# LayerNorm boundaries in another order: weight units of the modulation behind the statistics, four at each boundary, and the next two weight units split ahead

## The chip, the core and the metric

The kernel runs on one core of a Trainium2 chip. Its engines are TensorE (PE; its weight loads are shown as PEld), VectorE (DVE), ScalarE (ACT), GpSimd (POOL) and SyncE (SP, which issues most of the weight transfers). Each of them works through its own list of instructions in the order in which the list was written; the lists meet through semaphores. The metric is the device time in microseconds (us) of one execution.

## What is computed

The reference runs a trunk of four layers over 288 token columns: a prompt of 256 tokens and eight samples of 4. Cut to what matters:

```python
for i in range(DEPTH):                      # DEPTH = 4, d = 1024
    mod = sc @ w_ada[i] + b_ada[i]          # sc = silu(c): 9 vectors, w_ada[i] is 1024 x 6144
    sh1, sc1, g1, sh2, sc2, g2 = jnp.split(mod[:, None, :], 6, axis=-1)
    h = x * (1 + sc1) + sh1
    out = mixer(i % 3, h)                   # 0: gating MLP, 1: gated recurrence, 2: latent attention
    x = layer_norm(ALPHA * x + g1 * out, ln1_g[i], ln1_b[i])
    h = x * (1 + sc2) + sh2
    x = layer_norm(ALPHA * x + g2 * squared_relu_mlp(h, w1[i], w2[i]), ln2_g[i], ln2_b[i])
```

All is in 32-bit floats. The layers 0 and 3 have the gating MLP as their mixer, layer 1 the recurrence, layer 2 the attention.

## The kernel before

Activations lie with the 1024 features on partitions, in 8 chunks of 128, and the 288 tokens along the free dimension. A large matmul is done as three (`mm3`, L271 to L276): each operand is split into a high part and a low part, and high x high, low weight x high and high x low are added up in PSUM. So before a product the activation needs `Hi` and `Lo`, and each weight needs `hi` and `lo`.

Weights come in units of 1 MB: 1024 rows by 256 columns. `set_plan` fixes the order of all units. `load_next` issues a unit's transfer on SP into one of five `raw` buffers, and buffers are given back in the order of the plan only. `pump_` splits a unit in pieces of 1024 columns: ScalarE writes `hi` (L229), VectorE writes `lo` (L230). There are three pairs of `hi` and `lo`. `run_units` multiplies: a pair of units gives four output tiles. At the start of a stage (`inter=True`) the first two units are multiplied chunk by chunk of the activation, so that the matmuls of chunk 0 can start as soon as chunk 0 of `Hi` and `Lo` is there.

The modulation's matrix `w_ada` (24 MB a layer) also goes through the `raw` buffers, in 24 units a layer (each 1 MB): `ada` units and `adh` units. A unit is four matmuls of 32 columns by 512 (`ada_step`, L476), straight from `raw` without a split; the trace shows two records for each matmul, eight for a unit. After a group of units the sum is copied from PSUM by ScalarE (`adas`), turned by small matmuls on TensorE (L497 or L511) and added to a bias by VectorE. Where the units of the modulation stand in TensorE's list is set by three things: when their buffer must be free, the flag `hold`, and `fence`, a matmul behind which they must stand. Before the change `fence` is the last weight matmul ahead of a LayerNorm, and `ada_need` forces groups at certain places (ahead of the output projection of a mixer, and behind a boundary).

A boundary (`boundary`, L697) is the LayerNorm between two stages; there are seven, and a last one with the output (`store_y`). From the last matmul of a stage it goes: VectorE adds the residual to the last chunk of `Z`, ScalarE squares it, four matmuls with a constant matrix give mean and mean square over the features (`stats`, L611 to L614), ScalarE and VectorE make the reciprocal root (`rstd`: `va`, logarithm, exponential, and one correction step, L633 to L635). Then for each chunk VectorE subtracts the mean (L646) and multiplies (L649), ScalarE and VectorE write `Hi` (L661, L663) and a 32-bit copy `hf`, and VectorE writes `Lo` (L669). The scheduler of the language orders the instructions by dependencies and priority; `issue_after` adds a dependence without data, and `low` lowers a priority.

Of the kernel before, what the change touches and what calls it, by code (L numbers as in the profile page):

```python
# [11 lines left out]
AF = mybir.ActivationFunctionType  # L12
# [34 lines left out]
FENCE = 1  # L47

# [3 lines left out]
class Net:  # L52
    def __init__(s, ctx, tc, I, O, layers):
        s.tc, s.nc, s.I, s.O = tc, tc.nc, I, O
        s.layers = layers
        s.ctx = ctx
        P = lambda name, bufs=1, **k: ctx.enter_context(tc.tile_pool(name=name, bufs=bufs, **k))
        s.cst = P("cst")
        s.raw = P("raw", RAWB)
        s.hip = P("hip", HLB)  # L60
        s.lop = P("lop", HLB)
        s.acp = P("act")
        s.table = None
# [4 lines left out]
        s.paced = []  # L68

# [24 lines left out]
    def set_plan(s, plan):  # L94
# [7 lines left out]
        s.hold = True  # L102
        s.quiet = False
        s.rs_ins = None
# [65 lines left out]
    def pump(s, force=False):  # L170
        if s.quiet and not force:
            return False
        if s.rs_ins is not None and not force:
            with s.tc.issue_after(s.rs_ins), s.low(SPLIT_LATER):
# [96 lines left out]
    def mm3(s, out, w, x, first, last):  # L271

        mm = s.nc.tensor.matmul
        mm(out, w[0], x[0], start=first, stop=False)  # L274
        mm(out, w[1], x[0], start=False, stop=False)  # L275
        s.last_mm = mm(out, w[0], x[1], start=False, stop=last).ins  # L276
# [16 lines left out]
    def run_units(s, keys, x, evac, m0=0, nk=8, inter=False, kgroups=1, quiet=False):  # L293
# [4 lines left out]
        if inter:  # L298
# [3 lines left out]
            for k in range(nk):  # L302
                for m in range(4):
                    with s.after(k + 1):
                        s.mm3(pss[m][:, :T], s.wtile(ws[m // 2], k, m % 2), x(k), k == 0, k == nk - 1)
                    if k == nk - 1:
                        if m % 2:
                            s.wfree(ks[m // 2])
                        evac(m0 + m, pss[m])
# [288 lines left out]
    def stats(s, Z):  # L598
# [15 lines left out]
        nc.tensor.matmul(pq[:, :T], s.onesD, sq, start=False, stop=True)  # L614
        return pm, pq

    def rstd(s, pq, sub, out, n=T, mul=1.0):
# [3 lines left out]
        if sub is not None:  # L621
            nc.vector.scalar_tensor_tensor(v, pq, EPS, sub, op0=OP.add, op1=OP.subtract)
# [14 lines left out]
    def normalize(s, Z, pm, pq, each):  # L637
# [6 lines left out]
        if s.quiet:  # L644
            s.rs_ins, s.quiet = ins, False
        sub = lambda c: nc.vector.tensor_tensor(Z[:, c, :], Z[:, c, :], pm[:, :T], op=OP.subtract)  # L646
        for c in range(NCH):
            sub(c)
            nc.vector.tensor_tensor(Z[:, c, :], Z[:, c, :], rs, op=OP.mult)  # L649
            each(c)  # L650

    def make_h(s, Z, sub, c):
# [11 lines left out]
        nc.scalar.activation(hf[:, p], Z[:, c, p], AF.Identity, scale=A[:, c, 0:1], bias=B[:, c, 0:1])  # L664
        nc.vector.tensor_tensor(v(hf[:, q]), v(tp), bc(B), op=OP.add)
# [21 lines left out]
    def residual(s, Z, g, b, m):  # L687
# [5 lines left out]
        for c in range(NCH):  # L693
            nc.vector.tensor_scalar(s.AX[:, c, :], Z[:, c, :], ga[:, c:c + 1], ga[:, 8 + c:9 + c],
                                    op0=OP.mult, op1=OP.add)

    def boundary(s, sub, i):  # L697

        pm, pq = s.stats(s.Z)
# [21 lines left out]
    def ffn(s, i):  # L721
# [3 lines left out]
        with s.tc.tile_pool(name=f"ffn{i}", bufs=1) as fp:  # L725
# [16 lines left out]
            for h in range(2):  # L742
# [3 lines left out]
                if h == 0:  # L746
                    s.run_units(keys, y, lambda m, ps: s.gated(s.AX[:, m, :], ps, g, m), kgroups=2)
                else:
                    s.hold = True
# [899 lines left out]

    def before_out(s, i):  # L1650
        if i != s.layers[0]:
            s.ada_need(("adh", i, 4, 3))
            if i != s.layers[-1]:
                s.ada_need(("adh", i, 5, 3))
        s.hold = True

    def run(s):
# [3 lines left out]
        for n, i in enumerate(L):  # L1661
# [11 lines left out]
        s.set_plan(plan)  # L1673
        s.setup()
        s.late_setup()
        for n, i in enumerate(L):
            first, last = n == 0, n + 1 == len(L)
            s.hold = False
            if n:
                s.ada_need(("ada", i, 1, 7))  # L1680
                s.hold = True
# [11 lines left out]
            if first:  # L1693
                s.later_setup()
            if first or last:
                s.ada_need(("adh", i, 5, 3))
            if not last:
                i1 = L[n + 1]
                s.ada_need(("ada", i1, 0, 7))
                s.prep_ab(i1, 0, s.lnv(2, i), s.lnv(3, i))  # L1700
# [97 lines left out]
```

## Time and profile before

| | us |
|---|---|
| median of 3 runs | 1626.4 (1622.16 to 1628.55) |
| the profiled execution, its own time | 1626.94 |
| its span, first to last instruction | 1625.2 |
| TensorE busy in it | 1580.1 |
| VectorE busy | 1025.6 |
| ScalarE busy | 798.2 |

The span is that of the same execution as the trace, so rows of the trace are set against 1625.2, and 1.7 us lie around it. A busy time is the union of an engine's instructions; matmuls overlap, so on TensorE the distance from start to start says more than the length of one. A wait is the idle time of an engine ahead of an instruction, put down to what ended it.

### The profile page before, as it was taken

Reading aid. Unit: us, or ns where it says so; the run is one execution under the profiler, and the core shown is the slowest. Engines: PE = TensorE matmul, PEld = TensorE weight load, DVE = VectorE, ACT = ScalarE, POOL = GpSimd, SP = SyncE. Lnnn points to the kernel's source line nnn. Section 1 sums busy time; section 2 is a strip of 40 time slices with the busy share of each in tenths; the row PEclk is TensorE's granted clock in tenths of the full one; section 3 lists DMA queues with packets and bytes.
Section 4 is the critical chain, followed back from the end, with each engine's and each line's share of the span. In section 5 each row is a group of like instructions: output and inputs, shape, how many; then the busy total and the mean of one; then the engine's idle time right before and its main releaser. Section 6 shows DMA issues by size and latency. Waiting matters only on the chain.

```text
span 1625.2 us, 30504 instructions
## 1 busy us (share of the span) xinstructions
PE 1580.1 (97%) x12538; PEld 1402.2 (86%) x12538; DVE 1025.6 (63%) x2290; ACT 798.2 (49%) x1436; POOL 53.0 (3%) x70
## 2 busy tenths in 40 slices
PE   6999999999999989999999999999999999899997
PEld 2878899997989769999987676779999799799997
DVE  3567855656778786555676344586466775874655
ACT  2554643545777655345364453455254464553542
POOL 1000000000101100000002210000000000000000
PEclk9999999999999999999999999999999999999999
DMA  9977955458555868555465447696554766655531
GB/s 332 331 268 243 340 172 165 158 180 291 163 159 164 300 253 260 164 160 177 156 214 178 158 168 252 215 310 208 159 172 162 258 209 211 207 182 175 162 105 42
DMA packets 222717, 332.58 MB, mean 205 GB/s; under 512 B 7171, under 2 KB 196041, under 8 KB 213362
## 3 DMA queue, kind: packets, MB, share of 16 engines
q1 hardware_dynamic: 215954, 299.86, 55.6%
q0 software_dynamic: 6624, 30.78, 5.7%
q8 instruction: 98, 1.61, 0.4%
q14 instruction: 41, 0.34, 0.1%
HBM read 324.09 MB, written 6.53 MB: 203 GB/s over the span
## 4 chain that ended last, share of the span: by engine, by line
PE 90%; DMA 5%; DVE 3%; ACT 1%; issue 0%; SPq 0%; DVEq 0%; ACTq 0%
PE mm L274 24%; PE mm L276 23%; PE mm L275 23%; PE ada L476 5%; DMA raw<-in_w_ada 3%; PE mm L1408 2%; DMA raw<-in_ffn_w 1%; PE mx L1426 1%; PE mm L1462 1%; PE mx L815 1%; PE mx L1480 1%; PE mx L917 1%; PE mx L1430 1%; PE ada L530 1%; DVE lo L230 1%; PE mm L1508 1%
## 5 line engine op out<-in xcount | busy, mean ns | idle before, releaser
L230 DVE TENSOR_TENSOR lo<-raw,hi 128x1024 fp32r<-128x1024 f32 x360 | 433.2, 1221 | 166.5 <-ACT hi L229 166.0
L229 ACT ACTIVATE hi<-raw 128x1024 fp32r<-128x1024 f32 x360 | 370.6, 1053 | 264.1 <-PE mm L276 191.0
L274 PE MATMUL mm<-Hi,hi 128*128 128x288 f32 x1064 | 318.5, 300 | 1.8 <-ACT Hi L1161 0.9
L275 PE MATMUL mm<-Hi,lo 128*128 128x288 f32 x1064 | 316.7, 298 | 0.0
L276 PE MATMUL mm<-Lo,hi 128*128 128x288 f32 x1064 | 315.0, 298 | 0.0
L276 PE MATMUL mm<-FL,hi 128*128 128x288 f32 x1024 | 303.6, 297 | 0.0
L274 PE MATMUL mm<-FH,hi 128*128 128x288 f32 x1024 | 302.6, 296 | 0.0
L275 PE MATMUL mm<-FH,lo 128*128 128x288 f32 x1024 | 298.6, 292 | 0.0
L274 PEld LDWEIGHTS mm<-Hi,hi 128*128 128x128 f32 x1064 | 199.8, 188 | 19.6 <-issue 10.1
L274 PE MATMUL mm<-OH,hi 128*128 128x288 f32 x704 | 209.6, 299 | 2.7 <-ACT OH L661 2.7
L275 PE MATMUL mm<-OH,lo 128*128 128x288 f32 x704 | 208.8, 297 | 0.2 <-DVE lo L230 0.2
L276 PEld LDWEIGHTS mm<-Lo,hi 128*128 128x128 f32 x1064 | 199.5, 188 | 10.3 <-issue 8.4
L275 PEld LDWEIGHTS mm<-Hi,lo 128*128 128x128 f32 x1064 | 199.9, 188 | 9.4 <-issue 8.6
L276 PE MATMUL mm<-OL,hi 128*128 128x288 f32 x704 | 207.2, 297 | 0.0
L275 PEld LDWEIGHTS mm<-FH,lo 128*128 128x128 f32 x1024 | 195.2, 191 | 0.0
L274 PEld LDWEIGHTS mm<-FH,hi 128*128 128x128 f32 x1024 | 192.4, 188 | 0.0
L276 PEld LDWEIGHTS mm<-FL,hi 128*128 128x128 f32 x1024 | 191.9, 187 | 0.0
L737 ACT ACTIVATE r<-mm 128x288 f32<-128x288 f32 x128 | 52.3, 412 | 175.2 <-PE mm L276 159.0
L274 PEld LDWEIGHTS mm<-OH,hi 128*128 128x128 f32 x704 | 132.9, 189 | 5.5 <-ACT OH L661 3.6
L276 PEld LDWEIGHTS mm<-OL,hi 128*128 128x128 f32 x704 | 132.8, 190 | 4.3 <-issue 3.4
L275 PEld LDWEIGHTS mm<-OH,lo 128*128 128x128 f32 x704 | 133.2, 189 | 1.4 <-issue 0.8
L739 DVE TENSOR_TENSOR s<-r 128x288 f32<-128x288 f32 x128 | 58.1, 456 | 103.6 <-ACT r L737 103.5
(434 smaller groups left out, 2073.4 us busy)
## 6 DMA issues: line engine op xcount, KB each, us to landing
raw<-in_ffn_w SPq DMA_DIRECT2D x128, 1024.0 KB, 5.6
raw<-in_w_ada SPq DMA_DIRECT2D x88, 1024.0 KB, 5.6
raw<-in_a_w_in SPq DMA_DIRECT2D x16, 1024.0 KB, 9.2
raw<-in_b_w_in SPq DMA_DIRECT2D x16, 1024.0 KB, 8.5
raw<-in_w_ada SPq DMA_DIRECT2D x16, 512.0 KB, 10.0
raw<-in_a_w_out SPq DMA_DIRECT2D x8, 1024.0 KB, 5.9
St<-in_state_hgrn POOLq DMA_DIRECT2D x8, 512.0 KB, 6.4
out_hs_s<-St POOLq DMA_DIRECT2D x8, 512.0 KB, 4.1
```

The costliest lines, as they stand in the source:

```text
L229: nc.scalar.activation(hi[:, a:b], r[:, a:b], AF.Copy)
L230: nc.vector.tensor_tensor(lo[:, a:b], r[:, a:b], hi[:, a:b].bitcast(F32), op=OP.subtract)
L274: mm(out, w[0], x[0], start=first, stop=False)
L275: mm(out, w[1], x[0], start=False, stop=False)
L276: s.last_mm = mm(out, w[0], x[1], start=False, stop=last).ins
L476: nc.tensor.matmul(s.pa[32 * j:32 * j + 32, :], x, w, start=(k == 0), stop=(k == last), skip_group_check=True)
L530: mm = nc.tensor.matmul(pa[r0:r0 + 32, :], s.scT[:, 2 * kp + par, :], t[:, par, h, :], start=(kp == 0), stop=(kp == 3), skip_group_check=True)
L737: nc.scalar.activation(r, ps[:, :T], AF.Relu)
L739: nc.vector.tensor_tensor(sq, r, r, op=OP.mult)
L815: nc.tensor.matmul(pt[:, 128 * q:128 * q + 128], vt01[:, q, sl], s.wsT[:, c, :], start=True, stop=True)
L917: mm(pt[32 * b:32 * b + 32, 64 * hh + 32 * g:64 * hh + 32 * g + 32], k[:, hh, a:a + 32], q[:, hh, a:a + 32], start=True, stop=True, skip_g ...
L1408: tr(pt[:, 128 * n:128 * n + 128], lat[b][t // 8][:, t % 8, 128 * c:128 * c + 128], s.id)
```

## The change

- Modulation units at a boundary: `fence` becomes the last matmul of the statistics, and after each weight unit the last matmul of that unit. A counter `quota` lets four units go at a boundary (`FILL`), and then one for each weight unit that is done; `alim` bounds how far ahead they may run.
- The plan of units is laid out to fit: two weight units, four modulation units, and then one modulation unit after each weight unit in the mixers, after every second one in the MLP (`spread`). The groups that were forced ahead of the output projections of layers 1 and 2 are no longer there.
- `presplit` splits the next stage's first two weight units ahead of the statistics.
- `normalize`: three subtractions of the mean go right behind `va`, the others behind the reciprocal root; chunk 0 goes to its end ahead of the others; further splits wait for chunk 4 of `h`, and the residual copy `AX` for the last chunk.
- `run_units` at the start of a stage: for all chunks but the last, the two matmuls with `Hi` of all four tiles, then the one with `Lo`.
- The constants and tables that were made at the first boundary (`later_setup`) move into the first MLP.

```diff
+EARLY = 3
+AHEAD = 4
+FILL = 4
+SPACE = (1, 1, 1)
...
+    def presplit(s):
+
+        while s.nsplit < min(s.wdone + 2, len(s.wlist)):
+            s.reach(s.wlist[s.nsplit])
+            s.pump(force=True)
...
         s.wdone += 1
         del s.hl[key]
+        s.quota = max(s.quota, 0) + 1
+        s.fence = s.last_mm
         s.advance()
...
             for k in range(nk):
+                if k < nk - 1:
+                    for part in range(2):
+                        for m in range(4):
+                            with s.after(k + 1):
+                                s.mm3(pss[m][:, :T], s.wtile(ws[m // 2], k, m % 2), x(k), k == 0, False, (part,))
+                    continue
...
-        if s.ndone >= len(s.alist) or s.alist[s.ndone] >= s.nd or (s.hold and not force):
+        if s.ndone >= len(s.alist) or s.alist[s.ndone] >= s.nd or ((s.hold or s.quota < 1 or
+                                                                                s.alist[s.ndone] > s.alim) and not force):
             return False
+        s.quota -= 1
...
+        with s.tc.issue_after(s.va_ins):
+            for c in range(EARLY):
+                sub(c)
+        front, s.h_ins = ins, None
         for c in range(NCH):
-            sub(c)
-            nc.vector.tensor_tensor(Z[:, c, :], Z[:, c, :], rs, op=OP.mult)
-            each(c)
+            with s.tc.issue_after(front):
+                if c >= EARLY:
+                    sub(c)
+                nc.vector.tensor_tensor(Z[:, c, :], Z[:, c, :], rs, op=OP.mult)
+                each(c)
...
     def boundary(s, sub, i):
 
+        s.presplit()
         pm, pq = s.stats(s.Z)
...
+    def spread(s, w, a, first, n, step):
+
+        out, a = list(w[:first]) + list(a[:n]), list(a[n:])
+        for k, u in enumerate(w[first:]):
+            out.append(u)
+            if a and k % step == step - 1:
+                out.append(a.pop(0))
+        return out + a
+
     def before_out(s, i):
         if i != s.layers[0]:
             s.ada_need(("adh", i, 4, 3))
-            if i != s.layers[-1]:
-                s.ada_need(("adh", i, 5, 3))
+        s.hold = True
...
-                plan += s.merge(a, s.ada_units(i, 1), *R1) + s.merge(o, sc2 + ([] if last else g2), *R2)
-            fill = (g2 if first or last else []) + ([] if last else s.ada_units(L[n + 1], 0))
-            plan += s.merge(f[0] + f[1], fill, *R0[n]) + f[2] + f[3]
+                plan += s.spread(a, s.ada_units(i, 1) + sc2, 2, FILL, SPACE[i % 3]) + o
+            fill = g2 + ([] if last else s.ada_units(L[n + 1], 0))
+            plan += s.spread(f[0] + f[1], fill, 2, FILL, 2) + f[2] + f[3]
...
-            if FENCE:
-                s.fence = s.last_mm
             s.boundary(1, i)
-            s.hold = False
...
+            s.fence = s.last_stat
+            s.hold, s.quota = False, FILL
...
+            s.advance()
+            s.ada_need(("adh", i, 5, 3))
+            s.quota = 0
             s.rs_ins = None
             s.ffn(i)
             if not last:
-                if FENCE:
-                    s.fence = s.last_mm
                 s.boundary(0, i)
+                s.fence = s.last_stat
```

Three places in the instruction lists follow. The first is TensorE's list at the second boundary, that between the MLP of layer 0 and the recurrence of layer 1; `ada<-raw` are matmuls of modulation units, four to a unit, and `mx<-zs`, `mx<-sqs`, `mx<-Z` and `mx<-sq` are the statistics. Before:

```order
L611 MATMUL mx<-zs,con 128x288
L612 MATMUL mx<-sqs,con 128x288
L476 MATMUL ada<-raw,scT 32x512
L613 MATMUL mx<-Z,con 128x288
L614 MATMUL mx<-sq,con 128x288
L476 MATMUL ada<-raw,scT 32x512 x23
L274 MATMUL mm<-Hi,hi 128x288
```

The same place now:

```order
L639 MATMUL mx<-zs,con 128x288
L640 MATMUL mx<-sqs,con 128x288
L641 MATMUL mx<-Z,con 128x288
L642 MATMUL mx<-sq,con 128x288
L504 MATMUL ada<-raw,scT 32x512 x16
L294 MATMUL mm<-Hi,hi 128x288
```

The one unit matmul between the statistics is gone, and four units instead of six stand ahead of the first weight matmul. The second place is TensorE's list in the last part of the recurrence in layer 1, where the matmuls of the last pair of heads (`q,k`, `St,q`, `con,k`) follow one another and the weight matmuls have become few. Before:

```order
L476 MATMUL ada<-raw,scT 32x512
L969 MATMUL mx<-q,k 32x32 x8
L476 MATMUL ada<-raw,scT 32x512 x8
L982 MATMUL mx<-q,k 64x64 x4
L476 MATMUL ada<-raw,scT 32x512 x7
L274 MATMUL mm<-Hi,hi 128x288
L990 MATMUL mx<-q,k 128x128 x2
L998 MATMUL mx<-St,q 32x512 x4
```

The same place now:

```order
L1017 MATMUL mx<-q,k 32x32 x8
L294 MATMUL mm<-Hi,hi 128x288
L295 MATMUL mm<-Hi,lo 128x288
L1030 MATMUL mx<-q,k 64x64 x4
L1038 MATMUL mx<-q,k 128x128 x2
L1046 MATMUL mx<-St,q 32x512 x4
```

The units have gone from between the heads' matmuls. The third place is VectorE's list at the third boundary, that between the recurrence and the MLP of layer 1; `lo<-raw,hi` is a piece of a split, `Z<-gs,AX` the end of the residual sum of the last chunk, `Z<-Z,mx` a subtraction of the mean. Before:

```order
L573 TENSOR_TENSOR gs<-mm,modT_81 128x32
L230 TENSOR_TENSOR lo<-raw,hi 128x1024
L574 TENSOR_TENSOR Z<-gs,AX 128x32
L230 TENSOR_TENSOR lo<-raw,hi 128x1024
L646 TENSOR_TENSOR Z<-Z,mx 128x288
L622 SCALAR_TENSOR_TENSOR va<-mx,msq 128x288
L646 TENSOR_TENSOR Z<-Z,mx 128x288 x3
L633 SCALAR_TENSOR_TENSOR vl<-rs,va 128x288
L646 TENSOR_TENSOR Z<-Z,mx 128x288
L634 TENSOR_TENSOR vl<-vl,rs 128x288
L646 TENSOR_TENSOR Z<-Z,mx 128x288
L635 SCALAR_TENSOR_TENSOR rs<-vl,rs 128x288
```

The same place now:

```order
L601 TENSOR_TENSOR gs<-mm,modT_81 128x32
L241 TENSOR_TENSOR lo<-raw,hi 128x1024
L602 TENSOR_TENSOR Z<-gs,AX 128x32
L650 SCALAR_TENSOR_TENSOR va<-mx,msq 128x288
L674 TENSOR_TENSOR Z<-Z,mx 128x288 x3
L661 SCALAR_TENSOR_TENSOR vl<-rs,va 128x288
L662 TENSOR_TENSOR vl<-vl,rs 128x288
L663 SCALAR_TENSOR_TENSOR rs<-vl,rs 128x288
L684 TENSOR_TENSOR Z<-Z,rs 128x288
L706 TENSOR_TENSOR hs<-Z,A_90 128x32
L707 TENSOR_TENSOR Hi<-hs,B_92 128x32
```

`va` is now ahead of the subtractions, none of them stands between the three steps of the root, and chunk 0 runs on to `Hi`; of the two pieces of a split that stood in the chain, one is still there.

## Rows read from the trace of the kernel before

**Rows 1.** The page, part 1: busy us (share of the span) xinstructions.

```profile
PE 1580.1 (97%) x12538; PEld 1402.2 (86%) x12538; DVE 1025.6 (63%) x2290; ACT 798.2 (49%) x1436; POOL 53.0 (3%) x70
```

**Rows 2.** Windows over the seven boundaries, modulation units alone: length, busy (xrecords), clock, DMA.

```profile
376.30:387.27 10.97, 6.53 (x48) 1.48 (x48) 1.00 0.93 321
...
1390.29:1404.08 13.79, 4.89 (x32) 0.96 (x32) 0.94 0.73 241
...
sum 80.90, PE 45.53 PEld 9.73; mean PE 6.50 PEld 1.39
```

**Rows 3.** Timeline of TensorE, second boundary: start, length, instruction, xcount [idle before <-releaser].

```profile
377.36 1.04 PE L476 MATMUL ada<-raw,scT 128*32 128x512 f32 x2
378.34 0.75 PE L613 MATMUL mx<-Z,con 128*128 128x288 f32 x2
...
379.50 4.49 PE L476 MATMUL ada<-raw,scT 128*32 128x512 f32 x38
386.28 1.06 PE L476 MATMUL ada<-raw,scT 128*32 128x512 f32 x8 [2.28 <-DMA raw<-in_w_ada]
387.27 0.40 PE L274 MATMUL mm<-Hi,hi 128*128 128x288 f32 x1
```

**Rows 4.** Timeline of VectorE and ScalarE at the second boundary.

```profile
377.12 0.19 DVE L574 TENSOR_TENSOR Z<-gs,AX 128x32 f32<-128x32 f32 x1
379.57 0.45 DVE L646 TENSOR_TENSOR Z<-Z,mx 128x288 f32<-128x288 f32 x1 [2.26 <-ACT msq L641]
379.94 0.45 DVE L622 SCALAR_TENSOR_TENSOR va<-mx,msq 128x288 f32<-128x288 f32 x1
...
382.91 0.45 DVE L635 SCALAR_TENSOR_TENSOR rs<-vl,rs 128x288 f32<-128x288 f32 x1
...
384.13 0.60 ACT L661 ACTIVATE Hi<-Z,B,A 128x256 fp32r<-128x256 f32 x1 [2.73 <-DVE Z L649]
...
384.85 0.19 DVE L663 TENSOR_TENSOR Hi<-hs,B 128x32 fp32r<-128x32 f32 x1
```

**Rows 5.** Timeline of TensorE: one unit in the stream of weight matmuls.

```profile
389.37 0.30 PE L274 MATMUL mm<-Hi,hi 128*128 128x288 f32 x1
389.50 0.29 PE L275 MATMUL mm<-Hi,lo 128*128 128x288 f32 x1
389.72 1.06 PE L476 MATMUL ada<-raw,scT 128*32 128x512 f32 x8
390.72 0.40 PE L276 MATMUL mm<-Lo,hi 128*128 128x288 f32 x1
```

**Rows 6.** Timeline of ScalarE at the third boundary, of TensorE at the seventh.

```profile
588.99 1.06 ACT L229 ACTIVATE hi<-raw 128x1024 fp32r<-128x1024 f32 x1 [3.83 <-DMA raw<-in_ffn_w]
...
1399.91 1.07 PE L497 MATMUL mx<-con,adas 128*128 128x18 f32 x8 [0.71 <-ACT adas L494]
1403.67 0.61 PE L274 MATMUL mm<-OH,hi 128*128 128x288 f32 x1 [2.70 <-ACT OH L661]
```

**Rows 7.** Windows: length, busy of PE, PEld, DVE, ACT, POOL, granted clock, DMA.

```profile
1013.40:1023.50 10.10, 9.25 (x31) 5.42 (x30) 3.48 (x10) 3.98 (x10) 0.00 (x0) 0.50 0.86 331
1402.50:1409.20 6.70, 5.53 (x23) 5.53 (x24) 5.13 (x27) 6.70 (x14) 0.00 (x0) 0.50 1.10 349
```

**Rows 8.** The mixers' last parts: windows of units alone, then timelines.

```profile
539.87:572.00 32.13, 10.03 (x64) 2.04 (x64) 1.00 0.93 336
1001.17:1041.39 40.22, 15.25 (x64) 2.10 (x64) 0.87 0.75 267
...
543.95 0.42 DVE L943 TENSOR_TENSOR k<-k,tot 128x256 f32<-128x256 f32 x1
...
545.50 0.61 PE L990 MATMUL mx<-q,k 128*128 128x128 f32 x4
...
1017.09 0.60 ACT L494 ACTIVATE adas<-ada 128x512 f32<-128x512 f32 x1 [10.16 <-PE ada L476]
...
1017.88 0.61 PE L274 MATMUL mx<-vh,hi 128*128 128x288 f32 x1 [0.85 <-ACT vh L1576]
```

More of the change, by code (lines that the diff above doesn't have):

```diff
@@ L102, in set_plan @@
         s.hold = True
+        s.quota = 99
+        s.alim = -1
         s.quiet = False
-        s.rs_ins = None
+        s.rs_ins = s.rs_act = None
         for n, (kind, key, src) in enumerate(plan):
@@ L268, in preload, with mm3 @@
         s.table = "le"
-    def mm3(s, out, w, x, first, last):
+    def mm3(s, out, w, x, first, last, parts=(0, 1)):
         mm = s.nc.tensor.matmul
-        mm(out, w[0], x[0], start=first, stop=False)
-        mm(out, w[1], x[0], start=False, stop=False)
-        s.last_mm = mm(out, w[0], x[1], start=False, stop=last).ins
+        if 0 in parts:
+            mm(out, w[0], x[0], start=first, stop=False)
+            mm(out, w[1], x[0], start=False, stop=False)
+        if 1 in parts:
+            s.last_mm = mm(out, w[0], x[1], start=False, stop=last).ins
     def psmm(s):
@@ L613, in stats @@
         nc.tensor.matmul(pm[:, :T], s.onesD, Z[:, c, :], start=False, stop=True)
-        nc.tensor.matmul(pq[:, :T], s.onesD, sq, start=False, stop=True)
+        s.last_stat = nc.tensor.matmul(pq[:, :T], s.onesD, sq, start=False, stop=True).ins
         return pm, pq
@@ L644, in normalize @@
         if s.quiet:
-            s.rs_ins, s.quiet = ins, False
+            s.rs_ins, s.rs_act, s.quiet = ins, None, False
         sub = lambda c: nc.vector.tensor_tensor(Z[:, c, :], Z[:, c, :], pm[:, :T], op=OP.subtract)
+        with s.tc.issue_after(s.va_ins):
+            for c in range(EARLY):
+                sub(c)
+        front, s.h_ins = ins, None
         for c in range(NCH):
-            sub(c)
-            nc.vector.tensor_tensor(Z[:, c, :], Z[:, c, :], rs, op=OP.mult)
-            each(c)
+            with s.tc.issue_after(front):
[3 more added lines that the diff above has]
+                each(c)
+            if s.h_ins is not None:
+                if c == 0:
+                    front = s.h_ins
+                if c == AHEAD:
+                    s.behind = (s.h_ins, s.h_act)
+                if c == NCH - 1:
+                    s.behind_all = s.h_ins
+        if s.rs_ins is ins and s.h_ins is not None:
+            s.rs_ins, s.rs_act = s.behind
     def make_h(s, Z, sub, c):
@@ L692, in residual @@
         nc.vector.tensor_scalar(ga[:, 8:], b, m, ALPHA, op0=OP.subtract, op1=OP.mult)
-        for c in range(NCH):
-            nc.vector.tensor_scalar(s.AX[:, c, :], Z[:, c, :], ga[:, c:c + 1], ga[:, 8 + c:9 + c],
-                                    op0=OP.mult, op1=OP.add)
+        with s.tc.issue_after(s.behind_all), s.low(2 * SPLIT_LATER):
+            for c in range(NCH):
+                nc.vector.tensor_scalar(s.AX[:, c, :], Z[:, c, :], ga[:, c:c + 1], ga[:, 8 + c:9 + c],
+                                        op0=OP.mult, op1=OP.add)
     def boundary(s, sub, i):
+        s.presplit()
         pm, pq = s.stats(s.Z)
@@ L747, in ffn @@
                     s.run_units(keys, y, lambda m, ps: s.gated(s.AX[:, m, :], ps, g, m), kgroups=2)
+                    s.later_setup()
                 else:
-                    s.hold = True
+                    s.before_end(i)
                     s.z_start()
@@ L1678, in run @@
             s.hold = False
+            s.alim = s.idx[("adh", i, 4, 3)]
             if n:
-                s.ada_need(("ada", i, 1, 7))
-                s.hold = True
+                s.quota = FILL
+                s.advance()
             s.rs_ins = None
@@ L1688, in run @@
                 s.bias_means()
-            if FENCE:
-                s.fence = s.last_mm
             s.boundary(1, i)
-            s.hold = False
[L1693 to L1700, printed above, removed]
+            s.fence = s.last_stat
+            s.hold, s.quota = False, FILL
+            s.alim = s.idx[("adh", i, 5, 3) if last else ("ada", L[n + 1], 0, 7)]
+            s.advance()
+            s.ada_need(("adh", i, 5, 3))
+            s.quota = 0
             s.rs_ins = None
```

26 lines of the change are left out of this document (17 added, 9 removed).

## The prediction

> **What bounds the kernel now.** I read the page first. TensorE is busy 97% of the span, VectorE 63%, ScalarE 49% [rows 1], so a gain can only come out of the few stretches in which TensorE waits, or out of work that it does at a bad place. No matmul is added or removed by the change. It moves the modulation's units of 1 MB about and reorders VectorE at the seven boundaries. So I cut the trace into three kinds of place: the boundaries, the steady streams, and the last parts of the two long mixers ("tails"), where weight matmuls have run out.
>
> The boundaries, from the first matmul of the statistics to the first weight matmul that is followed by others (at the first of them, from the units just ahead), take 80.9 us together [rows 2]. Six of the seven hold 48 records of units, which are 6 units, and the seventh holds 32, so 40 units stand in them. At the second boundary one sees why TensorE waits: the units run back to back, 38 records in 4.49 us or 0.9 to 0.95 us a unit, then the list holds one more unit whose transfer has not landed, and 2.28 us go by, though chunk 0 of `Hi` was complete at 385.04, before the 386.28 at which that unit starts [rows 3, 4]. At the third, ScalarE stands 3.83 us ahead of a split whose weights are late, with the squares for the statistics behind it [rows 6].
>
> In the stream a unit costs more. From the start of the weight matmul ahead of it (389.50) to that of the one behind it (390.72) are 1.22 us; without it that would be one step of the stream, 0.13 us (389.37 to 389.50) [rows 5]. So **a unit in the stream costs 1.09 us**, all exposed.
>
> **The boundaries.** How long will one last now? I take the second and go along its chain [rows 3, 4].
> - The residual of the last chunk ends at 377.31 (377.12 + 0.19). The third matmul of the statistics needs that, yet starts at 378.34, since a quarter of a unit stands ahead of it. It is behind the statistics now: 0.9 us earlier.
> - `va` starts at 379.94, one subtraction (379.57) after it could have. That subtraction is now behind it: 0.4 us.
> - From `va` to the end of the root are 3.4 us, with subtractions between the three steps, each step otherwise waiting for its predecessor: I take 0.5 us.
> - The root ends at 383.36, chunk 0 of `Hi` is complete at 385.04 (384.85 + 0.19), with three operations for other chunks between. In the new list there are none; the multiplication (0.45) and ScalarE's `Hi` (0.60) make about 1.1 us: 0.6 us.
>
> That is 385.04 - 2.4 = 382.6, or 6.4 us from 376.30. Into it go the statistics (2.1 us) and four units of 0.9 us, which fill it nearly. At the third, fifth and seventh boundary a piece of a split of about 1 us still stands on VectorE between two steps of the residual; I give these 7.4 us. Together 4 x 6.4 + 3 x 7.4 = 47.8 us.
>
> The old 80.9 us want two corrections: four weight matmuls stand inside the third (-0.5), and behind the seventh the clock is at half [rows 7] for 5.6 us of matmuls from 1403.67 on (+2.5, if the shorter wait no longer lets it fall). 82.9 - 47.8 = 35.1 us. Against it: 40 units were inside, 28 will be, and 12 go into streams at 1.09 us, 13.1 us. Two groups of turning matmuls of 1.0 us [rows 6] and one small matmul (0.3) also leave the first and seventh: 2.3 us. **The boundaries give 35.1 - 13.1 - 2.3 = 19.7 us.** Bounds: if the chain stays as long as it is (385.04 - 376.30 = 8.7 us each) 60.9 us are left in place of 47.8 and the gain is 6.6; if the clock's share and the piece on VectorE go well, 22.
>
> **The tails.** Sixteen units leave them, 8 in each. There they occupy TensorE 10.03 and 15.25 us [rows 8], more than 16 x 1.09, as some stand in pieces (a quarter of a unit takes as long as a whole one, 1.04 us [rows 3]) and some at half clock [rows 7]. With them go four groups of turning matmuls, 1.0 us each. All of it comes back in streams and behind boundaries: 16 x 1.09 + 4 x 1.0 = 21.4 us. What the tails get shorter is not in the trace; it lies between 0 (TensorE then waits instead) and the whole 29.3 us.
> - Recurrence: the units fill gaps in a chain through VectorE, but overfill them. `k` is ready at 544.37, its matmul starts at 545.50 behind a run of units [rows 8]: 1.1 us late. Counting four such places and the two ScalarE copies and bias sums in the closing chain, I take 4.5 us.
> - Attention: ScalarE stands 10.16 us ahead of the copy `adas`, with the splits of the attention's output behind it, until 1017.09; the matmuls wait for these splits [rows 8]. Eight heads follow at some 1.2 us each on VectorE, with pieces of units among them. I take 13 us, near the whole.
>
> **The tails cost 21.4 - 17.5 = 3.9 us.**
>
> **The rest.** In layer 3 four units stand back to back at 0.9 and are spread at 1.09: 0.7 us. In the new order five units of the mixers are cut in two by other matmuls, and each piece costs a whole unit's time: 0 to 5 us; some stand among matmuls that wait for VectorE, so I take 3. "High parts first" I cost at nothing: the old list already had the four pairs with `Hi` of chunk 0 ahead of its `Lo`, and TensorE takes 12 matmuls of 0.13 us for a chunk, 1.6 us, while ScalarE makes one in two operations of 0.6. If ScalarE were late by its third job, the copy of the modulation, that is 0.6 us at four boundaries. `presplit` adds no operation; its cover is the last unit of the stage, and its price is the 1 us counted above. In the plan the next MLP's units now stand ahead of the modulation's, so the wait of rows 6 should go; if it did not, it is back with 3.8 us at two boundaries. SP issues as many transfers as before, only in another order, and none of its waits stands in the sum; a weight unit lasts 48 matmuls or 6.3 us, and with a modulation unit beside it that is 2 MB in 7.4 us, 280 GB/s, less than the 349 GB/s that a window shows [rows 7].
>
> **The sum.** 19.7 - 3.9 - 0.7 - 3 = 12.1 us. The profiled execution took 1626.94, half a us from the median: 1614.8, **1615 us**, 0.7% less.
>
> **Rivals.**
> - *The tails just wait* (ends slower). If the chains of the tails run on VectorE and ScalarE at their own pace, taking units out of TensorE's list only bares waits, and the 17.5 us don't come: 1632.5. The place is the stretch of 540 to 572 and of 1001 to 1041; it decides once the two get shorter by less than 5.4 us together. For it: VectorE's chain there is one of short dependent steps. Against it: the 10.16 us on ScalarE, whose end is a unit's.
> - *The clock falls in the tails.* TensorE's granted clock is at half, 1.2 GHz, from 1013.4 to 1023.5 after a stretch of small transposes and units, and from 1402.5, in a wait of 2.70 us [rows 6, 7]; the 2.28 us at the second boundary didn't lower it, its window shows 1.00 [rows 2, 3]. With units gone from the tails, they hold less for TensorE. Each fall of 6.7 us costs half of it in what TensorE does there; two more, 7 to 8 us: 1623. The Trainium skill's page "TensorE: Matmul & The Clock Gate", section "HAM oscillation — how this bites in real kernels", speaks against the change in this: idle stretches between bursts of matmuls set the engine back to half rate, paid anew each time. By that rule the tails would lose the clock; the trace agrees at 1402.5 and doesn't at the second boundary.
> - *The chain of the boundary stays.* If the order on VectorE was not what set its pace, 1615 + 13 = 1628. The first two items above are plain in the rows, so I give it little.
> - *The tails give all* (29.3 in place of 17.5): 1603.
>
> **Chances.** Forecast 0.56 (its own range 1608 to 1622), all of the tails 0.18, chain stays 0.09, clock 0.08, tails wait 0.09. What this kernel's measurement can tell from no change is about 0.5%, 8 us: below 1618.3 or above 1634.5. Two thirds of the forecast and the fourth rival lie below, in all 0.58; of the tails' rival half and a part of "chain stays", where pieces of splits come late too, lie above, 0.08; the rest is 0.34. The range runs from the whole of the tails, 1602, to the other rivals, 1630.
>
> **What would show it.** Each boundary from the first statistics matmul to the first weight matmul 6.4 us (7.4 at the third, fifth, seventh), with 32 records of units and no wait for `w_ada` or `ffn_w`; `va` ahead of any subtraction; the first weight matmul released by ScalarE's `Hi`. The tails: no unit in them, matmuls with `vh` starting some 2 us after the last transposes' copies at most, a clock that falls no more often than before. Units in streams at 1.09 us. It would be wrong if boundaries kept 8 us or more, if TensorE's waits in the tails grew by what the units took, or if units in the stream waited for their transfers.

## The result, and the profile after

The changed kernel is slower: 1634.25 us median of 10 runs (1632.8 to 1637.45) against 1621.56 (1620.19 to 1628.55), a ratio of 1.0073 (0.95 interval 1.0059 to 1.0087; the two medians alone give 1.0078). The forecast was 1615, with a range of 1602 to 1630, and the time lies above it. The profiled execution took 1632.95 us, its span is 1631.2; that of before, on which the sum was made, 1625.2.

The page of after, part 1, stands beside [rows 1]:

```profile
PE 1580.3 (97%) x12538; PEld 1402.3 (86%) x12538; DVE 1026.6 (63%) x2290; ACT 801.4 (49%) x1437; POOL 53.2 (3%) x70
```

TensorE's busy time is the same to 0.2 us, so its idle time is longer by nearly all of the 6.0 us between the spans. The boundaries first, as [rows 2]: windows of units alone over the seven boundaries (length, busy of PE and PEld, clock, DMA):

```profile
154.28:160.84 6.56, 3.64 (x32) 0.94 (x32) 1.00 0.79 225
377.41:383.96 6.55, 3.64 (x32) 0.94 (x32) 1.00 0.96 283
593.73:600.92 7.19, 3.64 (x32) 0.94 (x32) 1.00 0.75 239
...
1402.87:1410.07 7.20, 3.64 (x32) 0.94 (x32) 1.00 0.75 244
sum 49.65, PE 25.48 PEld 6.56; mean PE 3.64 PEld 0.94
```

They are near what was forecast: 6.55 to 7.2 us but for the sixth with 8.27, and 49.65 in sum against 47.8. The second one, TensorE beside [rows 3], then VectorE beside [rows 4]:

```profile
379.06 0.70 PE L642 MATMUL mx<-sq,con 128*128 128x288 f32 x2
379.69 3.64 PE L504 MATMUL ada<-raw,scT 128*32 128x512 f32 x32
383.96 0.40 PE L294 MATMUL mm<-Hi,hi 128*128 128x288 f32 x1 [0.63 <-ACT Hi L705]
```

```profile
379.88 0.46 DVE L650 SCALAR_TENSOR_TENSOR va<-mx,msq 128x288 f32<-128x288 f32 x1 [1.46 <-PE mx L642]
...
382.32 0.46 DVE L663 SCALAR_TENSOR_TENSOR rs<-vl,rs 128x288 f32<-128x288 f32 x1
...
383.53 0.19 DVE L707 TENSOR_TENSOR Hi<-hs,B 128x32 fp32r<-128x32 f32 x1
```

`va` is ahead of every subtraction, the root takes from 379.88 to 382.78, chunk 0 is complete 0.94 us later, and TensorE waits 0.63 us in all. So the loss is in the stages between. Their lengths from both traces, from one first weight matmul to the next statistics:

| | before | after | difference |
|---|---|---|---|
| seven boundaries | 76.55 | 49.65 | -26.9 |
| MLP of layer 0, 1, 2 | 209.2, 208.4, 208.0 | 216.6, 215.3, 216.2 | +22.4 |
| MLP of layer 3 | 206.5 | 206.1 | -0.4 |
| recurrence | 200.8 | 209.8 | +9.0 |
| attention | 244.1 | 244.7 | +0.5 |
| gating MLP of layers 0, 3 (from 94.90) | 62.5, 99.2 | 59.4, 103.6 | +1.3 |

(In the first row a boundary ends with its first weight matmul, as in all that follows; so before's sum is 76.55 where the prediction, to the first that others follow, had 80.9.) The sum of the differences is 5.9 of the 6.0 us between the spans. The recurrence and the attention were to get shorter by what their tails held, and didn't. Windows from the same matmul ahead of the tail to the boundary, recurrence and attention, before and then after (length, busy of PE, PEld, DVE, ACT, POOL, clock, DMA):

```profile
537.73:588.08 50.35, 49.49 (x401) 39.26 (x401) 37.48 (x90) 26.38 (x59) 2.93 (x4) 1.00 0.78 276
991.91:1062.36 70.45, 69.60 (x499) 50.85 (x493) 39.68 (x104) 25.80 (x56) 0.00 (x0) 0.93 0.68 243
```

```profile
546.28:593.73 47.45, 39.72 (x321) 36.91 (x320) 38.31 (x87) 25.80 (x58) 2.93 (x4) 0.96 0.41 129
1005.72:1067.58 61.86, 55.29 (x419) 48.36 (x412) 39.50 (x99) 26.52 (x56) 0.00 (x0) 0.92 0.45 147
```

TensorE is busy 24.1 us less in the two together, but they are only 11.5 us shorter, 2.9 and 8.6: its idle time grew by 12.6. The streams ahead of the tails got longer by more than that, 11.9 us in the recurrence and 9.1 in the attention. In the recurrence's tail TensorE now does this (windows as above), and the timeline shows the end of the wait:

```profile
560.00:570.50 10.50, 10.49 (x72) 9.57 (x70) 6.81 (x12) 6.08 (x14) 2.91 (x4) 1.00 0.33 119
570.50:575.02 4.52, 0.00 (x0) 0.00 (x1) 3.92 (x9) 0.82 (x3) 0.02 (x1) 1.00 0.72 208
575.36:578.77 3.41, 3.41 (x17) 3.41 (x16) 0.48 (x3) 0.00 (x0) 0.00 (x0) 0.50 0.00 0
```

```profile
575.02 0.40 PE L294 MATMUL mm<-Hi,hi 128*128 128x288 f32 x1 [4.53 <-ACT Hi L1209]
```

With the units gone the scheduler has drawn matmuls of the output projection into their gaps. At 570.50 those whose input is ready are used up, and for 4.5 us TensorE waits for the last chunks of `Hi`, which VectorE and ScalarE make; then its granted clock is 0.50, 1.2 GHz, for 3.4 us. The other new thing is in the mixers' streams: there five units are cut in pieces by other matmuls. One of them, in the recurrence:

```profile
455.29 0.40 PE L297 MATMUL mm<-Lo,hi 128*128 128x288 f32 x1
455.62 1.04 PE L504 MATMUL ada<-raw,scT 128*32 128x512 f32 x2
456.33 0.59 PE L965 MATMUL mx<-q,k 128*32 128x32 f32 x32
456.72 1.10 PE L504 MATMUL ada<-raw,scT 128*32 128x512 f32 x6
```

### The profile page after: what moved, and what is told of

Same layout as the page of the kernel before. It is cut to its first block, busy times and chain, and to the rows that moved or that the text cites. A ratio compares the mean times of both kernels' runs of the same rounds, so it can differ in the third digit from the quotient of the medians.

```text
span 1631.2 us, 30568 instructions
## 1 busy us (share of the span) xinstructions
PE 1580.3 (97%) x12538; PEld 1402.3 (86%) x12538; DVE 1026.6 (63%) x2290; ACT 801.4 (49%) x1437; POOL 53.2 (3%) x70
## 4 chain that ended last, share of the span: by engine, by line
PE 87%; DVE 6%; DMA 3%; ACT 2%; issue 1%; SPq 0%; POOL 0%; DVEq 0%; ACTq 0%; POOLq 0%
PE mm L294 23%; PE mm L297 22%; PE mm L295 22%; PE ada L504 4%; DMA raw<-in_w_ada 2%; PE mm L1456 1%; DVE lo L241 1%; PE mx L1474 1%; PE mm L1510 1%; PE mx L1528 1%; PE ada L558 1%; PE mx L863 1%; PE mx L965 1%; PE mx L1478 1%; PE mm L1556 1%
## 5 line engine op out<-in xcount | busy, mean ns | idle before, releaser
L297 PE MATMUL mm<-Lo,hi 128*128 128x288 f32 x1064 | 297.4, 298 | 0.0
L297 PEld LDWEIGHTS mm<-Lo,hi 128*128 128x128 f32 x1064 | 193.8, 189 | 8.6 <-issue 7.5
L297 PE MATMUL mm<-OL,hi 128*128 128x288 f32 x704 | 195.1, 296 | 0.0
L294 PEld LDWEIGHTS mm<-OH,hi 128*128 128x128 f32 x704 | 132.1, 188 | 11.9 <-issue 5.0
L297 PEld LDWEIGHTS mm<-OL,hi 128*128 128x128 f32 x704 | 128.0, 188 | 1.9 <-issue 1.7
```

## The experiments

Each ratio is to the kernel before, on the same chip; the changed kernel's is 1.0073.

**Both kernels again.** Unchanged, for second traces.

> The kernel before, unchanged, for a second trace. Theory A (the profiled execution of before lay some 5 us above the usual one because the granted clock fell behind the seventh boundary): this execution takes about 1621 us where that fall is missing, and the seventh boundary is about 10.5 us long in place of 13.8. Rival (the 5 us are spread, transfers being a little slower everywhere): about 1621 us too, with the same seventh boundary and each stage a little shorter.

> The changed kernel, unchanged, for a second trace. Theory A (its loss lies in the same stages in each execution): the same lengths of stages within 1 us but for those with a fall of the granted clock; the gating MLP of layer 0 is 59.4 us with the fall near 120 us and 54.2 without it. Rival (the loss comes from more falls of the clock, spread at random): stages differ by 3 us and more, at other places.

The kernel before took 1622.97 us, 4 less than the execution on which the sum was made. 3.7 of it is the gating MLP of layer 0. Windows from 94.90 to its statistics, before, then before again:

```profile
94.90:157.37 62.47, 61.31 (x408) 49.97 (x407) 47.19 (x126) 32.07 (x58) 0.54 (x1) 0.95 0.69 228
```

```profile
94.90:153.65 58.75, 57.59 (x405) 46.47 (x403) 46.77 (x125) 31.49 (x57) 0.54 (x1) 1.00 0.74 239
```

The clock's fall near 122 us (1.2 GHz for 6.8 us) is missing. The seventh boundary and the fall behind it are there as before (14.0 us), so theory A had the place wrong. At the second boundary the wait for the last unit is there again, 2.42 us at 382.70, and this time the clock is at half for 3.4 us behind it (384.0), where the prediction had read that such a wait doesn't lower it. The changed kernel again took 1634.34: recurrence 209.9, attention 244.7, the MLPs within 0.3 us, and only the sixth boundary differs by more than 1 us (9.8). So its loss lies where it lay, as theory A had it.

**The old order, the new plan.** VectorE's order at the boundary undone, and with it the holding back of further splits and of the residual copies.

```diff
-        with s.tc.issue_after(s.va_ins):
-            for c in range(EARLY):
-                sub(c)
...
         for c in range(NCH):
-            with s.tc.issue_after(front):
-                if c >= EARLY:
-                    sub(c)
+            sub(c)
```

> The changed kernel, with VectorE's order at the boundaries as it was (each chunk's subtraction, multiplication and end in turn, no early subtractions, the residual copies not put behind). Theory A (the order on VectorE sets the length of a boundary, and the change won its time there): boundaries of about 8.7 us in place of 6.6 to 7.2, seven times 2 us, so about 14 us slower than the changed kernel: ratio to the kernel before 1.016. Rival (four units and the statistics fill the boundary, whatever VectorE's order): 1.007, as the changed kernel.

1.0259 (1.0228 to 1.0290), 30 us slower than the changed kernel. The boundaries take 72.2 us in place of 49.65: the order, with what is held back, does set their length once four units stand in them. The rest lies in the stages behind them, and there the clock falls more often. The second boundary's wait in the timeline, then windows behind the second and fourth:

```profile
392.76 0.37 PE L294 MATMUL mm<-Hi,hi 128*128 128x288 f32 x1 [4.27 <-DVE Hi L692]
```

```profile
393.60:397.01 3.41, 3.41 (x17) 3.41 (x16) 3.41 (x19) 3.41 (x8) 0.00 (x0) 0.50 1.08 402
...
840.80:847.60 6.80, 5.83 (x24) 5.86 (x25) 6.80 (x35) 6.80 (x14) 0.00 (x0) 0.50 0.61 236
```

Behind six of the seven boundaries the clock is at half for 3.4 to 6.8 us; from 60 to 1600 us it is there 61 us against 24 in the changed kernel. In the kernel before, with boundaries as long but six units in them, it fell behind one [rows 7], in its second trace behind two.

**The new order, the old plan.** `normalize`, `run_units`, the holding back of splits and residual copies taken over, all else as before.

> The kernel before with the new order at the boundaries alone (VectorE's order, the high parts first, splits and residual copies held back); its plan of units, the six units of a boundary, the tails' units and the splits stay as they were, only that the scheduler now puts the sixth unit some 4 to 10 weight matmuls behind the others. Theory A (the order is what won time and the plan is what lost it): boundaries of some 7.3 us (statistics 2.3, five units of 0.95) and a sixth unit at 1.09 us behind, against 10.5, at five of the seven, less at those with ScalarE ahead of a late split: about 10 us faster than before, ratio 0.994. Rival (the transfer of the sixth unit is late by 2.3 us wherever it stands, and that wait only moves into the stream): 1.000.

1.0003 (0.9992 to 1.0015). At the second boundary the first weight matmul is early, and then the sixth unit is waited for:

```profile
377.52 4.49 PE L491 MATMUL ada<-raw,scT 128*32 128x512 f32 x38
381.94 0.40 PE L283 MATMUL mm<-Hi,hi 128*128 128x288 f32 x1
...
384.31 1.06 PE L491 MATMUL ada<-raw,scT 128*32 128x512 f32 x8 [1.17 <-DMA raw<-in_w_ada]
```

To their first weight matmul the boundaries take 61.8 us, 14.7 less than before, but the stages behind them give it back: against the second trace of before the last MLP is 4.6 us longer (210.5), the MLP of layer 2 3.5, the attention 3.3 (245.8), and 3.5 lie in the others. Five of the sixth units now stand in the streams, at some 1.1 us each, and the rival's wait is there; but these two are not all of it.

**Whole units.** The second to fourth matmul of a unit at a higher priority.

```diff
             for j in range(4):
...
-                nc.tensor.matmul(s.pa[32 * j:32 * j + 32, :], x, w, start=(k == 0), stop=(k == last),
-                                 skip_group_check=True)
+                with s.tc.high_priority(offset=1000) if j else nullcontext():
+                    nc.tensor.matmul(s.pa[32 * j:32 * j + 32, :], x, w, start=(k == 0), stop=(k == last),
+                                     skip_group_check=True)
```

> The changed kernel, with the second to fourth matmul of each unit at a higher priority, so that no unit of the mixers is cut in pieces by other matmuls. Theory A (each piece costs a whole unit's time): three units in the recurrence at 0.95 us, one in the attention in three pieces at 2.2 us and one in layer 3 at 1.05 us come back, about 6 us, ratio to the kernel before 1.0035. Rival (the pieces stand where TensorE would wait for VectorE or ScalarE anyway): 1.007 as the changed kernel.

1.0063 (1.0042 to 1.0084): in the time not to be told from the changed kernel. In the stages of the trace theory A's gain is there: recurrence 207.0, attention 240.7, gating MLP of layer 3 102.5, 7.9 us less than after in these three. Layer 0's gating MLP, with the clock at half for 13.7 us near 120 us in this trace, is 3.0 us longer.

**Units back in the tails.** Three ways. First the plan and `before_out`, with `alim` raised by a group; then with whole units, and with `alim` such that the eight are held until the weight matmuls run out (this edit is shown, without the lines that keep units whole); then the same in the recurrence alone, the attention's in its stream.

```diff
             s.ada_need(("adh", i, 4, 3))
+            if i != s.layers[-1]:
+                s.ada_need(("adh", i, 5, 3))
...
-                plan += s.spread(a, s.ada_units(i, 1) + sc2, 2, FILL, SPACE[i % 3]) + o
...
+                    plan += s.spread(a, s.ada_units(i, 1), 2, FILL, SPACE[i % 3]) + s.merge(o, sc2 + g2, *R2)
...
-            s.alim = s.idx[("adh", i, 4, 3)]
+            s.alim = s.idx[("adh", i, 4, 3) if first or last else ("ada", i, 1, 7)]
```

> The changed kernel, with eight units each put back into the last parts of the recurrence and of the attention. Theory A (sixteen units at 1.09 us and three units in pieces cost 22 us in the streams, and the tails gave back only about 14): about 9 us faster than the changed kernel, ratio to the kernel before 1.002 (1.000 to 1.003), the recurrence's tail 4 us longer, the attention's 10 us longer, streams of the two mixers 11 us and more shorter each. Rival (the loss is in the streams' waits for transfers or in the clock, and units cost the same wherever they stand): 1.007 as the changed kernel.

1.0056 (1.0035 to 1.0076): no test of the recurrence's tail, since its units went ahead of it. They stand from 497 to 533 us, and TensorE again waits 5.5 us for `Hi`. In the attention they stand late, from 1026.8 us on, 209.7 us into the stage.

> The changed kernel with whole units (as in the run of whole units) and with eight units each put back into the last parts of recurrence and attention, held until the weight matmuls there have run out; four units at each boundary as in the change. Theory A (16 units cost 1.09 us each in streams, in the tails only the 3.5 and 10 us by which those got shorter): 18 us less in streams, 13 us more in the tails, 5 us faster than the changed kernel with whole units: ratio to the kernel before 1.003. Rival (the tails' chains run at their own pace and take the units for nothing): 1.006 - 0.011 = 0.995.

0.9994 (0.9985 to 1.0003), between the two. In the attention the eight units stand 211.6 to 228.6 us into the stage. The waits of its chain of small matmuls, 5.4 us from 171 to 199 us into it, are ahead of that and stay. In the kernel before they stand from 182.9 us on, among that chain.

> The changed kernel with whole units and with eight units held back into the last part of the recurrence alone; those of the attention stay in the streams as in the change. Theory A (the recurrence's tail takes its units for nearly nothing: its stage lost 5 us though 4 units more stand in it, while the attention's stage grew by 9 us with 4 units more): nearly all of the 0.7% between the two runs before comes from the recurrence, ratio to the kernel before 0.997 to 1.000. Rival (both tails take their units at half price): half of the gain is missing, 1.003.

0.9988 (0.9973 to 1.0002): 0.75% or 12 us faster than with whole units, from eight units in the recurrence alone. Windows over recurrence and MLP of layer 1, with whole units and then with the tail filled:

```profile
387.81:594.85 207.04, 198.87 (x2188) 175.48 (x2188) 162.55 (x385) 144.21 (x291) 16.93 (x22) 0.98 0.61 195
602.05:817.93 215.88, 215.10 (x1613) 206.83 (x1614) 130.99 (x245) 98.73 (x152) 0.00 (x0) 1.00 0.64 210
```

```profile
386.88:588.73 201.85, 199.99 (x2228) 174.76 (x2228) 162.65 (x387) 145.57 (x293) 16.93 (x22) 1.00 0.68 221
595.91:806.25 210.34, 209.29 (x1572) 205.18 (x1573) 130.43 (x243) 98.26 (x151) 0.00 (x0) 1.00 0.60 196
```

```profile
571.55 0.40 PE L294 MATMUL mm<-Hi,hi 128*128 128x288 f32 x1 [0.86 <-ACT Hi L1210]
```

Four units more stand in the recurrence, and it is 5.2 us shorter; the MLP is 5.5 shorter by the four that left it. The wait for `Hi` is 0.86 us in place of 4.5, and the clock stays at 1.00 where it was 0.98. For the attention the two runs say that it is one whether its eight stand in its streams or behind its chain; neither puts them into the chain's waits.

**The empty tail filled with other work.** Whole units, and 32 matmuls of a unit's shape from data at hand, their result not used, in the recurrence's tail: work is added.

```diff
+        if i % 3 == 1:
+            pd = s.ps.tile([128, 512], F32, name="ada", tag="ada")
+            with s.tc.issue_after(s.last_mm):
+                for u in range(8):
+                    for j in range(4):
...
+                            s.nc.tensor.matmul(pd[32 * j:32 * j + 32, :], s.scT[:, u, :], s.con[:, :512],
+                                               start=True, stop=True, skip_group_check=True)
```

> The changed kernel with whole units (as in the run of whole units), and in the last part of the recurrence eight units' worth of extra matmuls (32 of 32 columns by 512, from data that is already there, result not used), where the kernel before had its eight units: work that is added, no transfer and no other instruction. Theory A (that stretch is a chain on VectorE and ScalarE in which TensorE has nothing to do, and when it is empty the granted clock falls behind it): 7.5 us of work are added and the time stays, or gets 1 to 3 us shorter as the two falls of the clock near 552 and 576 us are gone: ratio to the kernel before 1.004 to 1.007. Rival (units in the tail delay the chain at about half their length, as the prediction had it): about 4 us slower than with whole units, 1.009.

1.0055 (1.0042 to 1.0068) against 1.0063. Windows over the recurrence, all instructions and then the added ones alone:

```profile
387.62:594.35 206.73, 203.13 (x2252) 175.31 (x2253) 162.82 (x385) 144.31 (x291) 16.93 (x22) 1.00 0.61 195
...
387.62:594.35 206.73, 7.72 (x64) 1.76 (x64) 1.00 0.61 195
```

7.7 us of work make the stage 0.3 us shorter, theory A's value. Both falls of the clock in it are gone, the wait for `Hi` is 1.48 us in place of 4.52, and without the added matmuls TensorE is busy 3.5 us less (203.13 - 7.72 against 198.87 with whole units).

**Without the early splits.** `s.presplit()` taken out of `boundary`.

> The changed kernel without the splitting of the next stage's first two weight units ahead of the statistics; they are split when the scheduler comes to them. Theory A (it costs what the prediction counted, a piece of a split between two steps of the residual at the third, fifth and seventh boundary, and is worth nothing): these three boundaries 6.6 us in place of 7.2, ratio to the kernel before 1.006. Rival (it is what keeps ScalarE free of a late split there): a split stands between statistics and first matmul again, boundaries of 8 to 10 us, ratio 1.010 or more.

1.0153 (1.0132 to 1.0174), 13 us slower, and neither theory's way: the boundaries keep their lengths (7.19 at the third), but the stages behind them grow, the recurrence to 216.3 us, the gating MLP of layer 3 to 107.6, as splits now stand among the chunks of the first matmuls. One of the waits behind the second boundary:

```profile
389.48 0.54 PE L295 MATMUL mm<-Hi,lo 128*128 128x288 f32 x2 [0.70 <-DVE lo L241]
```

**Whole units in the kernel before**, alone and with the new order.

> The kernel before, with the second to fourth matmul of each unit at a higher priority, so that units stand whole: in the tails and between the statistics' matmuls, where they stood in pieces. Theory A (each piece costs a whole unit's time, and in the tails the kernel before pays for pieces): the recurrence's tail 3 us shorter, the attention's 2 to 4: ratio 0.996. Rival (the pieces lie in gaps in which TensorE waits anyway): 1.000.

0.9965 (0.9949 to 0.9980), theory A's value, though partly by luck. Against the second trace of before the attention takes 237.7 us for 242.5, a little more than expected, but the recurrence's tail is only 1.3 us shorter (49.1 for 50.4); the boundaries take 70.6 for 76.55, which no theory counted, and layer 0's gating MLP, with the clock at half for 13.7 us, is 7.1 longer.

> The kernel before with whole units and the new order at the boundaries, plan and number of units unchanged: the version that the runs so far point to. Theory A (with six units at a boundary it is their transfers and their 0.9 to 1.1 us each that set its length, not VectorE's order): nothing more than whole units alone gave, ratio 0.9965. Rival (with whole units the boundary of 8.9 us is set by VectorE's chain again, and the order takes 1 us off each of seven): 0.992.

0.9907 (0.9889 to 0.9926), median 1609.41: the rival's value, and its place. The boundaries take 61.8 us, 8.7 less than with whole units alone; the attention takes 238.3. This beats both kernels, and before by 0.9% or some 15 us, with before's own plan.

Set beside 0.9994, the run with whole units, the new order and both tails filled, it says that the rebuilt plan still costs 0.9%. 11.6 of the 11.9 us between the two traces lie in the attention (249.9 us with twelve units against 238.3 with ten, and the clock at half for 17.1 us against 6.8).

## Why the prediction was wrong

**The tails are the step that failed most:** "What the tails get shorter is not in the trace [...] I take 4.5 [...] I take 13 us", and from it "The tails cost 3.9 us" for all sixteen units. Between the two traces the tails got 11.5 us shorter up to their boundaries in place of 17.5, as TensorE's idle time in them grew by 12.6 us and, in the recurrence, its clock fell.

*The recurrence.* The pair with its tail empty and filled (1.0063 and 0.9988) shows 12 us for its eight units alone, where the step had 8 x 1.09 + 2.0 - 4.5 = 6.2. In their traces it is 10.7: the MLP gets 5.5 shorter and the recurrence's stream 6.2, and the tail with eight units in it gets only 1.0 longer (from the same weight matmul to the boundary 49.77 us for 48.76). The 4.5 was not a bad figure for how long units delay the chain there. What the step lacked is what an empty tail does: behind its gaps and its wait of 4.5 us the clock falls, with whole units twice for 3.4 us (552 and 576). Half of these 6.8 us, 3.4, is what a full clock gives back, an estimate that the 3.5 us of busy time in the run with added matmuls bears out. So 1.0 + 3.4 = 4.4 us is the delay by units. The added matmuls make the tail 1.2 us shorter (47.60), so their delay is 2.2. The units were what kept TensorE at full speed, and the sum costed that at nothing: "a clock that falls no more often than before" (the fall stood only among the rivals, with 0.08).

*The attention.* Its tail gave 8.6 us of the 13 taken. Much of that was pieces, not units: made whole, with plan and place as before, that stage alone wins 4.8 us. It then takes 237.7 us with ten units, against 240.7 with whole units and eight, all in the stream. Six more in the stream are 6 x 1.09 = 6.5 us, and the stage grew by 3.0, so taking eight whole units out of the tail gave back only about 3.5 (the two differ in the boundaries' order too, so this is an indication).

The rest of the 18.1 us between the forecast (-12.1) and the two traces (+6.0), term by term:

- *Boundaries:* order and length right, 49.65 for 47.8, 1.9 missing. What is shown beyond it: what the order is worth hangs on the units beside it, 1.9% on the new plan (1.0259 without it), nothing on the old plan (1.0003), 0.6% on the old plan with whole units (0.9965 to 0.9907).
- *Unit in the stream:* 1.08 to 1.09 us for each whole one in the stages after that doesn't wait for its transfer; right.
- *Cut units,* 3 us: mis-sized, 3.0 missing. Over 1.09 each they cost 0.99, 0.72 and 1.12 in the recurrence, 2.17 in the attention (three pieces), 1.04 in layer 3: 6.0.
- *Waits for transfers in the stream,* nothing in the sum: 2.9 us over 1.09 (1.2, 0.4 and 1.3 in the MLPs of layers 0 to 2), 2.0 of it idle ahead of four units by the list of waits. The first stands at 189.59, 0.56 us. The prediction's mean of 280 GB/s did not show it, and its own sign of being wrong, units that wait for their transfers, came.
- *Tails* between these two traces: 11.5 for 17.5, 6.0 missing.
- *Clock,* 2.5 us credited behind the seventh boundary: that fall is gone, and the last MLP is 0.4 us shorter with one group of turning matmuls (0.8) in it, so 1.3 is missing. The fall near 121 us is 10.2 long in place of 6.8; half of the difference is 1.7. (The new fall behind the recurrence's tail, 3.4 us at half clock, is in the term of the tails.)
- *`presplit`,* costed for what it adds: without it the streams behind the boundaries are 13 us longer. That didn't move the sum, since the sum took those streams as undisturbed.

Together 1.9 + 3.0 + 2.9 + 6.0 + 1.3 + 1.7 = 16.8 us; 1.3 us is not placed. So the tails are the largest term, a third of the miss, and not all of it.

The medians lie 12.7 us apart and the traces 6.0, since the trace of before was of an execution 5.4 us above the later median, and that of after 1.3 below its own. By the second trace most of the 5.4 is one fall of the clock in layer 0, so a sum made on an undisturbed execution would have ended nearer to 1610, further off. That fall varies: 6.8 us, none and 3.4 in three traces with units placed as before, 10.2 in each of after's two and with the old order, but none and 3.4 in two of its variants (the first with units in the tails, and the one without early splits), and 10.2 or 13.7 in all six with whole units. Whether the change makes it likelier is open; whole units seem to, which isn't explained.

*The rivals.* "The tails just wait" ended at 1632.5, 2 us from the median. Its condition, under 5.4 us from both tails, didn't hold (11.5), so it met the time by luck, with the help of other terms; but its mechanism is half of what happened, 12.6 us of new waits for 24.1 us of work that left. "The tails give all" fell with that. "The clock falls in the tails" is true of the recurrence: in all six traces of kernels without units there (after, after again, old order, the first way of putting units back, whole units, no early splits) the clock is at half for 3.4 to 10.2 us in that tail or right behind it; in the eight with units or added matmuls, never. It had 7 to 8 us for two falls; the one in after's trace costs about 1.7. The Trainium skill's page "TensorE: Matmul & The Clock Gate", section "HAM oscillation — how this bites in real kernels", has that idle stretches between bursts of matmuls set the engine back to half rate; the recurrence's tail and the old order with four units agree, with waits of 4.5 and 4.3 us, and the 0.63 us of after's boundaries didn't do it. "The chain of the boundary stays" fell with the 49.65 us.

One small slip stands in the chances: two thirds of 0.56 and the 0.18 make 0.55, not 0.58.

What stays open is the attention. Its eight units, held behind its weight matmuls, were worth no more than in its streams, and the traces show where they stood, behind the waits of the chain and not in them; that this is the reason was not tested. A run with them among the chain on the new plan, or with that tail filled with added work, was not tried. The clock is at half for 6.8 us or more in the attention's tail in each trace, with units in it and without.

## What to carry to other kernels

Before work is moved out of a stretch, ask what fills it afterwards: add matmuls whose result is not used, and if the time stays, the place was free and the work should stay there. Look first whether what stands there is in pieces; here keeping four matmuls together gave 0.35%, and with the new order 0.9%, where the rebuilt plan lost 0.7%. Two edits that act on one wait (a chain and a transfer) have to be tried apart and together, since each alone may show nothing.

## What the runs showed of the hardware

7.7 us of added matmuls in a waiting stretch cost nothing and kept the granted clock at 1.00. Waits of TensorE of about 4.3 to 4.5 us (from 570.50 in after, from 388.49 with the old order) are followed by 3.4 us or more at 0.50, at matmuls of 0.24 us from start to start in place of 0.13. A shorter wait is followed by it in one execution and not in another: at the second boundary of the kernel before 2.28 us without a fall, and 2.42 us with one. A quarter of a unit can take as long as the whole: two records 1.04 us, eight 1.06 [rows 3, 5].
